# A hybrid encoder layer on one core: mixer preparation queued between the last pairs of the first way down, the mixer's second norm started later, some two-operand VectorE/POOL work moved to VectorE, and the closing norms regrouped

## Chip, cores, metric

The kernel runs on one core of one Trainium2 chip. A core has TensorE (PE in the profile; PEld is its weight loads), VectorE (DVE), ScalarE (ACT), GpSimd (POOL) and SyncE (SP), which here only issues transfers. The metric is device time in microseconds of a whole execution, as the median of several runs.

## The reference

One layer of a streaming encoder for 1152 tokens (1024 of a new stream, eight running streams of 16) with 1024 features, all in float32:

```python
x = x + 0.5 * swiglu(rms_norm(x, norm_ffn1), w_ffn1_gate, w_ffn1_up, w_ffn1_down)
m = mixer(rms_norm(x, norm_mix), w_in, ..., w_out, s0, conv_buf, pool_buf, pos0, chunk)
x = x + m
x = x + 0.5 * swiglu(rms_norm(x, norm_ffn2), w_ffn2_gate, w_ffn2_up, w_ffn2_down)
y = rms_norm(x, norm_final)
```

`swiglu` is `(silu(x @ w_gate) * (x @ w_up)) @ w_down` with 2816 hidden features. The mixer projects its input into a gated delta rule of four heads (causal convolution, normalised keys and queries, a chunked triangular solve, a state) and four pooled groups, and multiplies the joined result by `w_out`. The states are outputs too.

## The kernel before

Features lie on the 128 partitions (eight tiles of 128, `KT`), tokens along the free axis, in three chunks: chunk 0 of 512 tokens, chunks 1 and 2 of 320 each. To keep float32 accuracy at the matmul's faster type, each operand is split into a high part (ACT, a cast) and a low part (the difference), and each product is three matmuls: high x high, high x low, low x high. Nearly all of them are issued in `Products.matmul` (line 58), the transposes in line 62, so that these two lines stand for all of PE's work.

The program runs in this order.

1. `half_step` (first feed-forward half): gate and up projections. Chunks 1 and 2 are multiplied by 2x2 blocks of weights with seven block products instead of eight (Strassen's form); the sums of blocks that this needs are made in `Blocks.piece`: with two sources POOL adds them (L282), with `more` POOL adds a second sum to the first (L286), ACT makes the high part (L287), VectorE the low part (L288). `Blocks.mark` is the last low part issued, and `tc.issue_after(Blocks.mark)` queues what VectorE does in its block behind that instruction in VectorE's queue (order alone, no wait). The pieces turn round in a ring of buffers.
2. `downs`, the way down: `down0` for chunk 0, then `down12` for chunks 1 and 2 in twelve pairs `(g, d)`: the groups g have 4, 3 and 4 units ("four-wide", "three-wide"), and each has four pairs. A pair is seven products: `fifth` (T1), B11, B21, the T4 of the pair before, T2, B22, T3. Its four blocks of weights are loaded by SP into raw buffers that are reused (`load`, L642 and L643). `add` (L654) accumulates a product into x on VectorE. Of a pair's seven pieces three are sums of two blocks, T1's with `more`. A generator `beside` is advanced three times in a pair, after B21, B22 and T3; before the change it carries only the final norm of chunk 0, in the second way down.
3. The mixer. `h_tiles(0)` and `scale_split` (L249 on ACT, L250 on VectorE) make chunk 0's scaled input; `rstd_of` and `rstd_parts` square it (L205, ACT), sum the squares (L209, VectorE) and take the root. Chunk 0's norm is the slow form (`fast=False`): two matmuls with a matrix of ones, a square root on ACT (L217), a reciprocal on VectorE (L218). The fast form (`rstd_rest`) sums by tiny matmuls, scales on VectorE (L231), takes the power -1/2 on POOL (L232) and spreads the result with matmuls that ACT copies out (L237).
   The order within the mixer is made by a planner at build time. Tasks have names such as `Ay0`: block A (chunk 0) or B (chunks 1 and 2), a letter, a head. `p`, `v`, `g` are projections, `w` and `y` prepare and invert the triangular matrix, `c` runs the chain of states, `m` is a pooled group, `o` multiplies by the output weights, `r` is the second norm (chunks 1 and 2). `rule(n, ...)` names what must be done before n. A list `fill` of projections and output products is worked off in its order, and a task at its head that isn't free yet stops it; the other tasks are taken when they are due: a step that yields t is due again after 1.35 t of the planned PE time. After that a scheduler puts each engine's instructions into an order of its own by priority and its estimate of when they are ready, so that work later in the program may run earlier.
   `load_mix` loads and splits a 128 x 1024 block of weights (L185 the high part on ACT, L186 the low part): the low part is VectorE's, but POOL's for the output weights (kind "o", sixteen blocks).
   The inverse's first part is a loop of thirty small VectorE steps (L1120, L1121); its last copies are in L1173. Output products are added to x in L1002.
4. The second half step and way down. In the last pairs `square` squares each finished tile of x (L1552, ACT) and sums (L1558, VectorE); the last square of a chunk is kept apart. After the last product `final(2)` and `final(1)` run step by step in turn: sums, power, spread, then eight scalings each: VectorE straight from PSUM (L1579), two of eight on POOL (L1577, after a multiplication by the weight on ACT, L1576), and each tile is stored by SP or ACT (L1583). `final(0)` runs beside the first pairs and scales in L1582.

Of the kernel before, what the change touches and what calls it, by code (L numbers as in the profile page):

```python
# [40 lines left out]
def trunk(ctx: ExitStack, tc: tile.TileContext, xin, s0, convst, poolst, cm_in, vec_in, small_in,  # L41
# [5 lines left out]
    class Products:  # L47
# [3 lines left out]
        def put(self, r, time):  # L51
            self.t += time

# [135 lines left out]
    def load_mix(src, kind):  # L189
        with tc.high_priority(offset=300):  # L190
            return load_unit(src, None, G if kind in "o" else V)
# [76 lines left out]
    class Blocks:  # L268


        def __init__(self, ring):
            self.gs, self.ring, self.n = Slots(), ring, 0

        def piece(self, *src, more=None):
# [5 lines left out]
            if len(src) == 2:  # L280
                t = self.gs.get("s", m)
                G.tensor_add(t, *src)  # L282
                src = [t]
# [328 lines left out]
    def down12(wd, gk, op0, beside, done):  # L612


        bl = Blocks(["O3", "O4", "O0", "O1", "O2"])
        gs, piece, product = bl.gs, bl.piece, bl.product
# [53 lines left out]
        for u, (g, d) in enumerate(units):  # L670
# [76 lines left out]
    def downs(wd, gk, src, done0=None, after=lambda c: (), done12=None):  # L747
# [65 lines left out]

    half_step(0, wg1, wu1, g_keep)
    downs(wd1, g_keep, xin)


    weights(("R0", "R1", "O5"), (("O2", "O3"), ("O4", "O6"), ("O0", "O1")))
    ms = Slots()
    mt = ms.get  # L820
    WIDE = HIST + 512 + NB * (HIST + NS)
# [6 lines left out]
    ms.place(region("A4"), ("raw", WIDE, 2), ("ss", 32, 2), ("sss", 32, 2), ("ucar", 60, 1), ("cst", 288, 1))  # L828
# [4 lines left out]
    ms.place(region("R2"), ("eglS", 32, 1), ("osbs", P, 1), ("scout", 288, 1), ("Vcs", 16, 2), ("Ucs", 16, 1), ("tus", 16, 1))  # L833
    ms.place(region("R3"), ("big", 1024, 1))
# [35 lines left out]
    R = [mt("big", 512), rb[:, :320], rb[:, 320:]]  # L870
    ROWS = ((0, 1, 2, 0), (1, 0, 2, 1))

    def mix_block(blk, hb, extra, zrow):
# [471 lines left out]
        def part_of(w, h):  # L1345
# [42 lines left out]
            if w == "r":  # L1388
                sq = mt("z", 640)
                for c in (1, 2):  # L1390
                    rstd_of(c, pair(z2, sq[:, :320], sq[:, 320:]), R[c], True)
                yield 1
        return part_of

    def pair(acc, *sq):
# [3 lines left out]
        def get(tag):  # L1399
            if tag == "nacc":  # L1400
                return acc
            turn[0] += 1
            return sq[turn[0] % 2]
# [80 lines left out]
    rule("Am0", "Ar0")  # L1484
# [57 lines left out]
    def square(c, d):  # L1542
# [17 lines left out]
    def final(c):  # L1560
        o, n = CHUNKS[c]
        last = c > 0
        pool = (2, 5) if last else ()
        r = nt[c].get("nsq", n)
        root = rstd_rest(n, squares[c], r)
        next(root)
        if not last:
            yield
            yield
        yield  # L1570
        pr = yield from root
        yield
        for k in range(KT):
            x, w = xk(c, k), vec[:, 24 + k:25 + k]
            if k in pool:
                A.mul(x, x, w)  # L1576
                G.tensor_tensor(x, x, r, ALU.mult)  # L1577
            elif last:
                V.scalar_tensor_tensor(x, x, w, pr, ALU.mult, ALU.mult)  # L1579
            else:  # L1580
                with tc.issue_after(Blocks.mark):
                    V.scalar_tensor_tensor(x, x, w, r, ALU.mult, ALU.mult)  # L1582
            (A if last and (k in pool or c == 1 and k % 2) else SY).dma_start(y_out[:, o * KT + k * n:o * KT + (k + 1) * n], x)  # L1583
            yield

    downs(wd2, g_keep, x_keep, lambda d: square(0, d), final, square)


# [90 lines left out]
```

## Time and profile before

| | |
|---|---|
| median of 3 runs | 2175.2 us (2174.64 to 2175.72) |
| the profiled execution's own time | 2173.01 us |
| its span in the profile | 2171.2 us |
| instructions | 33111 |
| PE busy | 2121.9 us, 98% of the span |
| VectorE busy | 1525.1 us, 70% |
| ACT busy | 924.8 us, 43% |
| POOL busy | 607.1 us, 28% |
| mean granted TensorE clock | 0.996 |

Times in the profile are microseconds from the start of the span, those of single groups nanoseconds. A row of the timeline is: start, duration, engine, line, operation, tile written and tiles read, shapes, count, and in brackets how long the engine had idled and whose end released it. "Busy" of PE is modelled, as matmuls overlap; a hole in it is real, a busy PE need not be at its peak. The final stores and the closing of the program lie behind the last computing instruction, inside the span.

### The profile page before, as it was taken

To read this page: it belongs to the slowest core of one execution; us is meant where nothing else is said; L and a number is where in the kernel's file an instruction comes from. 1 tells how busy PE (TensorE), PEld (TensorE's weight loads), DVE (VectorE), ACT (ScalarE), POOL (GpSimd) and SP (SyncE) were. 2 spreads that over 40 slices of the span, in tenths; PEclk is the share of its full clock that TensorE was granted. 3 is DMA by queue.
4 is the path that set the end of the run, shared out by engine and by line. 5 is a ranking of instruction groups with operands and counts; after the bars stand their busy time and mean duration, and the time that the engine had idled before them with its cause. 6 is when DMAs were issued, how large, how long until landed. Compare 5 with 4: busy or idle time off the path is not lost.

```text
span 2171.2 us, 33111 instructions
## 1 busy us (share of the span) xinstructions
PE 2121.9 (98%) x12341; PEld 1914.9 (88%) x12341; DVE 1525.1 (70%) x2764; ACT 924.8 (43%) x1886; POOL 607.1 (28%) x532
## 2 busy tenths in 40 slices
PE   8999999999999999999999999999999999999997
PEld 7899999999889887787899988889999999987997
DVE  7966666677337887778687877786666668744776
ACT  7433333444213455545455445543433334422333
POOL 1433333351014421111111211243333334100443
PEclk9999999999999999999999999999999999999998
DMA  6333333464465622121222122433333347446572
GB/s 254 117 124 107 127 113 110 164 222 144 152 217 196 232 78 79 40 69 51 71 90 81 54 87 91 165 117 114 117 112 122 111 141 245 137 134 220 201 263 70
DMA packets 102673, 289.71 MB, mean 133 GB/s; under 512 B 16240, under 2 KB 24304, under 8 KB 102256
## 3 DMA queue, kind: packets, MB, share of 16 engines
q1 hardware_dynamic: 101360, 286.40, 39.2%
q8 instruction: 97, 1.59, 0.3%
q10 hardware_dynamic: 1152, 1.19, 0.2%
q14 instruction: 64, 0.52, 0.1%
HBM read 214.89 MB, written 72.66 MB: 132 GB/s over the span
## 4 chain that ended last, share of the span: by engine, by line
PE 80%; DVE 10%; DMA 4%; issue 2%; ACT 2%; POOL 2%; SPq 0%; DVEq 0%; POOLq 0%; ACTq 0%
PE ps_a L58 29%; PE ps_b L58 19%; PE ps_d L58 17%; PE ps_c L58 14%; DVE O L288 2%; DMA R<-in_wd 1%; DVE x L654 1%; DMA B<-g_keep 1%; POOL Q L282 1%; DMA O<-in_wd 1%; PE ps_b L62 1%; DVE A L1120 1%; DVE A L1121 1%; ACT O L287 1%; DMA x<-g_keep 1%
## 5 line engine op out<-in xcount | busy, mean ns | idle before, releaser
L58 PE MATMUL ps_a<-B,O 128*128 128x320 f32 x3040 | 506.4, 310 | 9.6 <-DVE x L654 6.1
L58 PEld LDWEIGHTS ps_a<-B,O 128*128 128x128 f32 x3040 | 463.2, 188 | 21.2 <-issue 6.6
L58 PE MATMUL ps_a<-A,O 128*128 128x320 f32 (+1 forms) x1952 | 423.8, 353 | 5.6 <-DVE O L186 2.1
L58 PEld LDWEIGHTS ps_a<-A,O 128*128 128x128 f32 x1952 | 328.7, 189 | 40.1 <-issue 3.5
L288 DVE TENSOR_TENSOR O<-Q,O 128x512 fp32r<-128x512 f32 (+1 forms) x238 | 209.0, 879 | 194.2 <-ACT O L287 193.4
L58 PE MATMUL ps_b<-A,O 128*128 128x512 f32 (+1 forms) x1128 | 263.6, 387 | 6.3 <-ACT O L287 5.6
L58 PEld LDWEIGHTS ps_b<-A,O 128*128 128x128 f32 x1128 | 207.7, 188 | 46.9 <-ACT O L287 5.8
L58 PE MATMUL ps_d<-A,O 128*128 128x512 f32 x1056 | 244.0, 391 | 2.2 <-DVE x L606 1.3
L58 PEld LDWEIGHTS ps_d<-A,O 128*128 128x128 f32 x1056 | 196.8, 188 | 48.2 <-issue 3.5
L287 ACT CAST O<-Q 128x512 fp32r<-128x512 f32 (+1 forms) x238 | 143.3, 605 | 225.5 <-POOL Q L282 58.3
L288 DVE TENSOR_TENSOR O<-R,O 128x512 fp32r<-128x512 f32 (+1 forms) x216 | 199.3, 927 | 34.9 <-ACT O L287 33.9
L58 PE MATMUL ps_d<-B,O 128*128 128x320 f32 (+1 forms) x1104 | 203.8, 330 | 6.1 <-DVE x L1002 4.0
L58 PE MATMUL ps_c<-A,O 128*128 128x512 f32 (+1 forms) x816 | 186.9, 377 | 0.9 <-DVE O L288 0.9
L58 PEld LDWEIGHTS ps_d<-B,O 128*128 128x128 f32 x1104 | 171.1, 188 | 16.8 <-DVE x L1002 6.4
L287 ACT CAST O<-R 128x512 fp32r<-128x512 f32 (+1 forms) x216 | 131.2, 611 | 127.9 <-PE ps_a L58 50.2
L282 POOL TENSOR_TENSOR Q<-R 128x512 f32<-128x512 f32 (+1 forms) x44 | 57.7, 1311 | 450.1 <-DMA R<-in_wd 285.3
L58 PEld LDWEIGHTS ps_c<-A,O 128*128 128x128 f32 x816 | 145.5, 188 | 25.0 <-DVE O L288 1.4
L185 ACT CAST O<-R 128x1024 fp32r<-128x1024 f32 (+1 forms) x86 | 85.9, 1010 | 183.7 <-PE ps_d L58 134.7
L58 PE MATMUL ps_c<-B,O 128*128 128x320 f32 x912 | 145.5, 311 | 0.0
L58 PEld LDWEIGHTS ps_c<-B,O 128*128 128x128 f32 x912 | 137.8, 189 | 0.3
L186 DVE TENSOR_TENSOR O<-R,O 128x1024 fp32r<-128x1024 f32 (+1 forms) x74 | 87.2, 1185 | 50.5 <-ACT O L185 29.8
L393 POOL TENSOR_TENSOR A<-A,A 128x512 fp32r<-128x512 f32 x44 | 72.7, 1652 | 162.1 <-ACT A L392 162.0
(311 smaller groups left out, 2982.7 us busy)
## 6 DMA issues: line engine op xcount, KB each, us to landing
g_keep<-x SPq DMA_DIRECT2D x98, 320.0 KB, 2.5
R<-in_wg SPq DMA_DIRECT2D x48, 512.0 KB, 3.8
R<-in_wd SPq DMA_DIRECT2D x48, 512.0 KB, 3.7
R<-in_wu SPq DMA_DIRECT2D x47, 512.0 KB, 3.6
g_keep<-A SPq DMA_DIRECT2D x44, 512.0 KB, 2.7
A<-g_keep SPq DMA_DIRECT2D x44, 512.0 KB, 5.5
B<-g_keep SPq DMA_DIRECT2D x56, 320.0 KB, 6.6
A<-g_keep SPq DMA_DIRECT2D x42, 320.0 KB, 4.9
```

Source lines behind the costliest of these rows:

```text
L58: self.put(nc.tensor.matmul(out, lhs, rhs, **k), n / 2400 + .003 if lhs.dtype == F32R else max(n, lhs.shape[-1]) / 600)
L62: self.put(nc.tensor.transpose(out, lhs, rhs), out.shape[-1] / 1200)
L185: A.copy(hi, raw)
L186: (e or V).tensor_sub(lo, raw, hi.bitcast(F32))
L282: G.tensor_add(t, *src)
L287: Blocks.high = A.copy(hi, src).ins
L288: Blocks.mark = V.tensor_sub(lo, src, hi.bitcast(F32)).ins
L393: G.tensor_sub(go[:, 1], sg, go[:, 0].bitcast(F32))
L654: V.scalar_tensor_tensor(xk(c, d), ps, by, xk(c, d), ALU.mult, ALU.add)
L1120: V.tensor_tensor(tu[:, :n, :w], xrow(slice(None), m), Uc[:, :, m:m + 1].to_broadcast([P, n, w]), ALU.mult)
L1121: V.tensor_tensor(Uc[:, :, m + 1:], Uc[:, :, m + 1:], tu[:, :n, :w], ALU.add)
```

## The change

Five parts, none of which adds or removes a product of the layer.

- **Sums of blocks in the way down.** `Blocks` has an engine `e` for the sum of two sources, POOL as before. `down12` sets it to VectorE, and to POOL from the load of a three-wide pair to the load of the next four-wide one. The `more` sum stays on POOL.
- **Mixer preparation.** A generator `prologue` is given to the first way down as its `beside`: it lets 25 steps pass, then makes chunk 0's scaled input tile by tile, each followed by its square (`step=1`), VectorE's part queued behind the latest piece, with 2, 3, 3, 1, 1 and 1 steps in between; what is left comes after the last pair. This norm now has the fast form. Its square's buffer is one of the `raw` slots in place of `z`.
- **Second norm.** `Ar0` must wait for `Ay0`, and `Am1` for `Ar0` (before, `Am0` for `Ar0` and `Ar0` for nothing). It is cut into steps, each due after a yield of 2, and has one square's buffer of its own (`sqr`).
- **Low parts of the output weights** are made by VectorE as all others.
- **The end.** The last products' chunks have their seven first squares summed as soon as chunk 2's last tile is done (`partial`); `finals` adds the eighth, takes both powers, then spreads and scales chunk 2 and then chunk 1, tiles 1, 4 and 7 on POOL, stores of odd tiles on ACT's queue and of even ones on SP's. `final0` waits three steps before its root and takes two steps per tile.

```diff
-            return load_unit(src, None, G if kind in "o" else V)
+            return load_unit(src)
...
-                G.tensor_add(t, *src)
+                self.e.tensor_add(t, *src)
...
         bl = Blocks(["O3", "O4", "O0", "O1", "O2"])
+        bl.e = V
...
+                bl.e = G if GROUPS[g2][1] == 3 else V
                 w = load(g2, d2, 6 if g2 == 0 else 10)
...
-        down12(wd, gk, op0, iter(after(0)), done12)
-
-        ends = [iter(after(c)) for c in (2, 1)]
-        while ends:
-            ends = [e for e in ends if next(e, e) is not e]
+        down12(wd, gk, op0, iter(after0()), done12)
+        ends()
...
+    def prologue():
+
+        for _ in range(25):
+            yield
...
+        hb0.extend(h_tiles(0))
+        R.append(mt("big", 512))
+        buf = [mt("raw", 512) for _ in range(2)]
+        norm = rstd_parts(0, lambda tag: buf[tag == "nsq"], R[0], step=1)
+        for k in range(KT):
+            with tc.issue_after(Blocks.mark):
+                scale_split(0, 1, *hb0, [k])
+                next(norm)
+            for _ in range((2, 3, 3, 1, 1, 1, 0, 0)[k]):
+                yield
+        yield from norm
+
     half_step(0, wg1, wu1, g_keep)
-    downs(wd1, g_keep, xin)
+    downs(wd1, g_keep, xin, after0=prologue)
...
             if w == "r":
-                sq = mt("z", 640)
                 for c in (1, 2):
-                    rstd_of(c, pair(z2, sq[:, :320], sq[:, 320:]), R[c], True)
-                yield 1
+                    for _ in rstd_parts(c, pair(z2, mt("sqr", 320)), R[c], step=1):
+                        yield 2
...
-    hb = {0: h_tiles(0)}
-    scale_split(0, 1, *hb[0])
-    rstd_of(0, pair(mt("raw", 512), mt("raw", 512), mt("z", 512)), R[0], False)
+    hb = {0: hb0}
...
-    rule("Am0", "Ar0")
+    rule("Ar0", "Ay0")
+    rule("Am1", "Ar0")
...
             squares[c].append(t)
+            if c == 2:
+                partial(2)
+                partial(1)
...
+    def final0():
+
+        r = nt[0].get("nsq", N0)
+        root = rstd_rest(N0, squares[0], r)
+        next(root)
+        for _ in range(3):
+            yield
+        yield from root
+        yield
+        for k in range(KT):
+            with tc.issue_after(Blocks.mark):
+                t = scaled(0, k, r, V)
+            SY.dma_start(*t)
             yield
             yield
...
+    def finals():
+
+        root = {}
+        for c in (2, 1):
+            ss = pt("d")[:, :3]
+            for i, a in enumerate(AT):
+                T.matmul(ss[:, i:i + 1], squares[c][1][:, a:a + P], ones[:, 0:1], start=True, stop=True)
+            summed = T.last
+            root[c] = const.tile([P, 4], F32, tag="rt", name=nm("rt"), bufs=3)[:, :3]
+            V.scalar_tensor_tensor(root[c], ss, 1.0 / D, sums[c], ALU.mult, ALU.add)
+            G.tensor_tensor(root[c], root[c], mhalf[:, :3], ALU.pow)
+        for c in (2, 1):
+            pr, r = pt("d")[:, :N], nt[c].get("nsq", N)
+            with tc.issue_after(summed):
+                for i, a in enumerate(AT):
+                    T.matmul(pr[:, a:a + P], root[c][:, i:i + 1].to_broadcast([P, P]), ident, start=True, stop=True)
+            A.copy(r, pr)
+            for k in range(KT):
+                pool = k in (1, 4, 7)
+                t = scaled(c, k, r if pool else pr, G if pool else V)
+                (A if k % 2 else SY).dma_start(*t)
...
-    downs(wd2, g_keep, x_keep, lambda d: square(0, d), final, square)
+    downs(wd2, g_keep, x_keep, lambda d: square(0, d), final0, square, finals)
```

`partial(c)` sums `squares[c][0]` with three tiny matmuls and scales the result on VectorE; `scaled` is a multiplication by weight and root, in one instruction on VectorE, or on ACT and then POOL.

More of the change, by code (lines that the diff above doesn't have):

```diff
@@ L52, in put @@
             self.t += time
+            self.last = r.ins
         def matmul(self, out, lhs, rhs, **k):
@@ L745, in half_step, with downs @@
         rest()
-    def downs(wd, gk, src, done0=None, after=lambda c: (), done12=None):
+    def downs(wd, gk, src, done0=None, after0=lambda: (), done12=None, ends=lambda: None):
         op0, stage = {}, []
```

54 lines of the change are left out of this document (25 added, 29 removed).

## The prediction

> **What bounds the kernel now.** I read the page first, then the table by stretches (busy time of each engine between two times) for the stages that the change touches, then the chain that ended last and the timeline inside them.
>
> ```profile
> PE 2121.9 (98%) x12341; PEld 1914.9 (88%) x12341; DVE 1525.1 (70%) x2764; ACT 924.8 (43%) x1886; POOL 607.1 (28%) x532
> ```
>
> TensorE (PE) is busy for 98% of the span, so no edit that leaves its matmuls alone can gain more than the holes between them. In the next two tables the first time is the width of the stretch and the second is PE's busy time in it; the time after the count is the weight loads', and then come VectorE (DVE), ACT and POOL. The first table is the way down of the two feed-forward halves after its first chunk (three rows each: four-wide, three-wide and four-wide group, roughly), the second the mixer.
>
> ```profile
> 653.00:694.00 41.00, 40.57 (x275) 40.05 (x274) 28.41 (x47) 14.44 (x25) 18.39 (x14) 1.00 0.48 160
> 694.00:738.00 44.00, 42.66 (x286) 41.59 (x285) 35.62 (x64) 19.94 (x38) 17.33 (x16) 1.00 0.84 308
> 738.00:788.00 50.00, 46.20 (x300) 45.21 (x299) 44.33 (x70) 21.68 (x37) 22.45 (x16) 0.97 0.28 91
> 1998.00:2047.00 49.00, 47.44 (x300) 45.24 (x300) 32.70 (x49) 15.37 (x27) 19.48 (x13) 1.00 0.64 215
> 2047.00:2104.00 57.00, 54.31 (x362) 53.11 (x363) 42.17 (x80) 17.49 (x35) 21.77 (x20) 1.00 0.74 266
> 2104.00:2153.00 49.00, 46.63 (x315) 45.72 (x314) 39.62 (x65) 22.91 (x43) 19.16 (x14) 1.00 0.15 44
> ```
>
> ```profile
> 800.00:877.00 77.00, 74.63 (x392) 60.73 (x391) 58.18 (x131) 47.12 (x100) 10.13 (x21) 1.00 0.23 66
> 877.00:932.00 55.00, 51.08 (x294) 42.68 (x293) 42.11 (x107) 26.39 (x78) 8.01 (x8) 0.97 0.14 44
> 932.00:1012.00 80.00, 76.68 (x410) 61.53 (x409) 65.04 (x166) 40.25 (x100) 16.90 (x19) 1.00 0.21 61
> 1012.00:1240.00 228.00, 226.71 (x1544) 209.77 (x1543) 178.25 (x539) 115.68 (x297) 38.30 (x72) 1.00 0.24 73
> 1240.00:1372.00 132.00, 124.20 (x848) 114.34 (x846) 98.96 (x258) 65.61 (x165) 21.58 (x21) 1.00 0.30 96
> ```
>
> Holes on PE, width less busy: 0.43 + 1.34 + 3.80 = 5.57 us in the first way down, 1.56 + 2.69 + 2.37 = 6.62 in the second, 2.37 + 3.92 + 3.32 + 1.29 + 7.80 = 18.70 in the mixer. In the same rows VectorE is the second engine: 44.33 of 50 us in the last pairs of the first way down. A hole can also cost a slower clock behind it (third column from the end):
>
> ```profile
> 738.00:745.00 7.00, 4.11 (x27) 3.59 (x25) 6.86 (x8) 2.42 (x5) 6.92 (x5) 1.00 0.27 107
> 745.00:749.50 4.50, 4.50 (x21) 4.50 (x22) 4.03 (x9) 3.12 (x5) 1.01 (x1) 0.62 0.45 125
> ```
>
> After 2.89 us idle within seven, PE runs the next 4.5 us at 0.62 of its clock: 4.5 x 0.38 = 1.71 us more, so the first way down has 7.28 us to win. The Trainium skill (TensorE: Matmul & The Clock Gate, What's actually happening) lets the clock fall only after an idle window of some 3.4 us; this trace shows it falling after less, so I follow the trace. By the page, the 1.71 us would not hang on this hole, and the estimate below would be 0.9 us smaller.
>
> **Way down: sums on VectorE.** What ends the waits there is told by the chain in the second way down (start, us, what), and the matmul that it releases:
>
> ```profile
> 2040.37 1.31 POOL Q L282
> ...
> 2043.80 1.39 DVE O L288
> ...
> 2046.90 0.40 DVE x L654
> ```
>
> ```profile
> 2048.44 3.75 PE L58 MATMUL ps_a<-B,O 128*128 128x320 f32 x24 [1.66 <-DVE x L654]
> ```
>
> Weights land, POOL adds two of them (1.31), ACT makes the high part, VectorE the low part (1.39), and the accumulation that PE needs (L654) stands behind all that in VectorE's queue. The groups of VectorE between 738 and 788 us show what the low parts cost beside POOL (count | busy us, mean ns of one):
>
> ```profile
> L288 DVE TENSOR_TENSOR O<-A,O 128x512 fp32r<-128x512 f32 x15 | 15.9, 1063 | 2.5 <-ACT O L287 2.3
> L288 DVE TENSOR_TENSOR O<-R,O 128x512 fp32r<-128x512 f32 x4 | 2.7, 678 | 0.0
> ```
>
> The same instruction takes 678 ns alone and 1063 where POOL adds at the time. Per pair of four-wide units three of POOL's four sums move (POOL's fourth and the three-wide group's sums stay): 24 per way down, 48 in all, at 0.68 us each on VectorE (the row of L288 alone: the same operation on the same shape) instead of 1.31 on POOL. A four-wide pair has 7 products x 4 tiles x 3 matmuls = 84, so the last stretch holds 300/84 = 3.6 pairs: 10.7 sums, 7.3 us more on VectorE. Given back: 15 x 0.385 = 5.8 us on that row alone; with three of four POOL sums gone, three quarters of it, 4.3. Net +3.0 on 44.33, against PE's own need of 50 - 3.80 - 1.71 = 44.5: VectorE and PE are level there. In the second way down VectorE has 32.70 + 7.3 = 40 and 39.62 + 7.3 = 47 before anything is given back, against 47.4 and 46.6 of PE: room, and the chain per pair is shorter by 0.63 (sum) and up to 0.7 (low part) of its 1.66 us wait. New waits: VectorE's sum now waits for the weights' DMA; behind it in its queue stand the accumulations L654 and the low parts of the next piece, and PE waits for both. POOL's remaining sum now waits for VectorE's. As PE waits for the same landing through the split anyway, I count this as nothing; if not, rival 3.
>
> Preparation of the mixer (eight scaled splits and squares) is now queued behind chosen pieces of the last four pairs, one tile at a time, where the scheduler had put it wherever it was ready; the work is the same. Its last two tiles come after the last pair. What covers these is this product, the last of the way down, and the one before it:
>
> ```profile
> 791.57 2.00 PE L58 MATMUL ps_a<-B,O 128*128 128x320 f32 x12
> ```
>
> Without that cover two tiles would cost 2 x (0.68 + 0.68) = 2.7 us. Square root and reciprocal of the first norm go; no wait in the list of PE's waits hangs on them for long: nothing. The first chunk's final scaling takes two steps per tile instead of one and so reaches into the three-wide group, where PE has 2.69 us of holes and VectorE 42.17 of 57: nothing, 0.5 at worst.
>
> I take half of 7.28 in the first way down (3.6; VectorE is level with PE), 60% of 6.62 in the second (4.0). Ends: all of both (13.9), and rival 1.
>
> **Second norm.** Two of PE's waits at the mixer's start are its pieces, one on a square's sum, one on POOL's power; one of its sums on VectorE is the third row; the last two are the end of the first pair's inverse and the first product of Am1, the task that now must wait for the norm:
>
> ```profile
> 803.73 0.83 PE L58 MATMUL ps_d<-ones,B 128*128 128x1 f32 x6 [1.08 <-DVE B L209]
> 818.18 0.94 PE L58 MATMUL ps_d<-ident,rt 128*128 128x128 f32 x6 [1.05 <-POOL rt L232]
> 801.30 0.49 DVE L209 TENSOR_TENSOR B<-B,A 128x320 f32<-128x320 f32 x1
> 874.70 0.41 DVE L1173 COPY B<-ps_b 64x256 f32<-64x256 f32 x1
> 932.39 0.94 PE L58 MATMUL ps_a<-A,O 128*128 128x512 f32 x3
> ```
>
> Gained: 1.08 + 1.05 = 2.1. Moved: 16 squares and 14 x 0.49 = 6.9 us of VectorE land between about 877 and 932, where PE has 3.92 us of holes; I charge 1.0 (0 to 3).
>
> **Output weights' low parts.** Sixteen go from POOL to VectorE. Durations (min/median/max ns), then three instructions of one small VectorE loop and a split beside it:
>
> ```profile
> L186 POOL TENSOR_TENSOR O<-R,O x12: 2357/2410/2938, 886.6 to 1342.9; 128x1024 fp32r<-128x1024 f32 x12
> L186 DVE TENSOR_TENSOR O<-O,O x14: 1161/1222/1227, 794.7 to 1283.3; 128x1024 fp32r<-128x1024 f32 x14
> 895.53 0.20 DVE L1120 TENSOR_TENSOR A<-A,A 128x36 f32<-128x36 f32 x1
> 896.81 2.39 POOL L186 TENSOR_TENSOR O<-O,O 128x1024 fp32r<-128x1024 f32 x1
> 896.92 2.33 DVE L1120 TENSOR_TENSOR A<-A,A 128x28 f32<-128x28 f32 x1
> ```
>
> A 0.20 us step is held for 2.33 by the split: it costs VectorE 2.1 us without running there. On VectorE it costs 1.22. Added: 16 x 1.22 = 19.5; given back at most 16 x 2.1 = 34, at least nothing. The stretches with these splits hold 3.92 + 3.32 + 7.80 = 15.0 us of PE's holes. That is what they can win, and not all of it hangs on VectorE: I take a third, 5.0; ends 15 and -10 (rival 1).
>
> **End.** Sums of squares in two parts, the first ahead; both powers before both spreads; scaling divided 10 to 6 between VectorE and POOL instead of 12 to 4; SP and ACT issue eight stores each instead of nine and seven.
>
> ```profile
> 2156.12 0.47 ACT L1552 ACTIVATE A<-x 128x320 f32<-128x320 f32 x1 [2.20 <-DVE x L654]
> 2158.24 1.41 PE L58 MATMUL ps_d<-ones,A 128*128 128x1 f32 x10
> 2160.84 1.65 PE L58 MATMUL ps_d<-ident,rt 128*128 128x128 f32 x6 [0.55 <-POOL rt L232]
> 2160.33 0.42 ACT L237 COPY A<-ps_d 128x320 f32<-128x320 f32 x1 [3.73 <-PE ps_d L58]
> 2160.79 1.47 DVE L1579 SCALAR_TENSOR_TENSOR x<-x,vec,ps_d 128x320 f32<-128x320 f32 x3 [0.93 <-ACT A L237]
> 2163.04 4.21 DVE L1579 SCALAR_TENSOR_TENSOR x<-x,vec,ps_d 128x320 f32<-128x320 f32 x9 [0.79 <-ACT A L237]
> ```
>
> The last square ends at 2156.59; six small sums at 1.41/10 each take 0.85 (2157.4); the other chunk's power is then done, so its spread follows: 0.94 to 1.65, I take 1.3 (2158.7); then ACT's copy and a start, 0.46. First scaling at about 2159.2 instead of 2160.79, and 10 x 0.49 (1.47/3) = 4.9 without the pause: last at 2164.1 instead of 2167.25. The stores start with the first scaling, and if it is they that set the end, its 1.6 us is all there is; if the last scaling sets it, 3.1. I take 1.6 (0.5 to 3.1).
>
> **Sum.** 3.6 + 4.0 + 2.1 - 1.0 + 5.0 + 1.6 = 15.3 us. The profiled execution took 2173.0 (span 2171.2 and 1.8 around it), so 2157.7; the median of the runs shown is 2175.2, 2.2 above the profiled one, so 2159.9. A difference of 0.2% (4.4 us) is about what a measurement of this kernel can tell from none.
>
> **Rivals.**
> 1. VectorE becomes the bound, and it is slower. Place: the last four-wide pairs of the first way down and the mixer's chains. If nothing is given back, VectorE has 44.33 + 7.3 = 51.6 us in a stretch of 50 (+1.6), and half of the 19.5 us of splits stand in PE's way (+9.8); less 1.6 at the end and 1.1 of the norm, +8.7: 2183.9. It decides where the low parts still average above 900 ns with the sums on VectorE. For it: 89% busy there already. Against: 678 against 1063 ns. The Trainium skill (Perfetto Trace Analysis, Optimizing Scalar/DVE Operations) speaks for it: work should leave a saturated DVE, to GPSIMD if need be. Chance 0.07.
> 2. The norm blocks the mixer's filler. It takes 18 steps, each followed by 2 x 1.35 = 2.7 us in the plan, 48.6 in all, from 874.70 to about 924; Am1 starts at 932.39, and a task that isn't free stops the whole list of filler. Ten us late would cost some 7 of PE's time and a clock dip of 1.7: 2168.6. Chance 0.10.
> 3. The way down gives nothing: VectorE waits on landings with L654 behind it, and the holes stay. 2159.9 + 7.6 = 2167.5. Chance 0.17.
> 4. Nearly all goes: 13.9 in the way down and 10 in the mixer instead of 7.6 and 5.0: 2159.9 - 11.3 = 2148.6, or somewhat lower. Chance 0.11.
> 5. Gains and new waits cancel: 2171 to 2179. The Trainium skill (the same page and section) holds that moving work between GPSIMD and DVE might not help, as they share a port. Chance 0.08.
>
> **How the numbers follow.** Forecast 0.47, at 2159.9. Faster: it and rivals 2, 3 and 4, less 0.03 for the slow tails of 2 and 3: 0.82. Same: 0.08 and those 0.03, 0.11. Slower: 0.07. The range 2146 to 2173 leaves out rival 1, half of 5 and a little of 4, under 0.2.
>
> **What the changed profile would show.** Right: L288 at 0.7 us in both ways down; PE's hole and clock dip at 742 gone; no wait of PE on L209 or L232 at 800 to 820; single steps of L1120 at 0.2 us throughout; the first scaling 1.6 us earlier behind the last product. Wrong: VectorE at 46 or more of 46 us in the last pairs; holes of several us before Am1; longer waits behind L186 on VectorE.

## The result and the profile after

The changed kernel takes 2148.84 us (median of 4 runs, 2147.65 to 2149.61), the kernel before beside it 2175.01 (4 runs, 2174.64 to 2175.72): ratio 0.9879, 95% interval 0.9862 to 0.9896. That is 26.2 us less; 15.3 were forecast. The profiled execution took 2148.53 us, its span is 2146.7. In the code after, lines have moved: the low part L288 is L289, the sum L282 is L283, the accumulation L654 is L656, the split L186 is L187, the loop L1120 is L1139, the products' L58 is L59.

The page's line of engines after. Against before TensorE has lost 5.6 us of busy time (2121.9 before), its holes shrink from 2171.2 - 2121.9 = 49.3 us to 30.4, VectorE is as busy as it was, and POOL has lost 109 us:

```profile
PE 2116.3 (99%) x12355; PEld 1914.3 (89%) x12355; DVE 1528.7 (71%) x2828; ACT 925.8 (43%) x1886; POOL 498.4 (23%) x471
```

The table by stretches of the two ways down after (start and end, width, then busy time of PE, its weight loads, VectorE, ACT, POOL, and the clock), to be held against the six rows of the prediction:

```profile
645.40:685.00 39.60, 39.60 (x270) 39.48 (x269) 33.99 (x57) 14.69 (x24) 4.81 (x4) 1.00 0.61 211
685.00:729.00 44.00, 43.41 (x294) 42.89 (x293) 33.22 (x61) 17.13 (x34) 16.64 (x16) 1.00 0.80 289
729.00:786.40 57.40, 56.47 (x375) 54.26 (x374) 54.30 (x98) 29.95 (x50) 6.48 (x6) 1.00 0.37 116
1989.00:2038.00 49.00, 49.00 (x339) 48.92 (x338) 42.01 (x73) 18.73 (x32) 10.70 (x8) 1.00 0.60 200
2038.00:2094.00 56.00, 54.04 (x356) 52.01 (x355) 44.51 (x83) 19.43 (x38) 15.65 (x14) 1.00 0.74 266
2094.00:2132.20 38.20, 38.20 (x264) 37.96 (x263) 31.45 (x60) 18.46 (x35) 2.60 (x2) 1.00 0.15 42
```

PE's holes: 1.52 us where 5.57 were, and 1.96 where 6.62 were. VectorE is at 54.30 of 57.40 us in the last pairs, 95%, and PE is held there for less than 1 us. The mixer in the same view:

```profile
787.00:862.00 75.00, 74.16 (x389) 59.70 (x389) 56.88 (x133) 43.79 (x92) 7.94 (x20) 1.00 0.24 72
862.00:917.00 55.00, 54.81 (x322) 46.22 (x321) 45.16 (x116) 30.38 (x86) 5.42 (x7) 1.00 0.15 49
917.00:995.00 78.00, 77.14 (x422) 63.34 (x421) 62.81 (x162) 41.03 (x102) 6.79 (x16) 1.00 0.21 63
995.00:1223.00 228.00, 227.27 (x1551) 209.97 (x1550) 181.91 (x552) 116.13 (x296) 27.32 (x68) 1.00 0.24 73
1223.00:1352.70 129.70, 123.30 (x835) 114.03 (x835) 97.52 (x262) 64.72 (x164) 8.68 (x15) 0.99 0.31 98
```

Holes of 9.0 us instead of 18.7. VectorE's busy time over these rows is 444.3 us, before 442.5. The rows are not quite the same work, as the preparation now lies ahead of them; the cleaner count is that of the low parts alone (b_olow, next section): over the whole mixer VectorE is busy for 445.5 us there and for 448.2 before. Sixteen splits were added, 19.5 us by the forecast's count, and all of it was given back by steps that are held no longer. In the small loop this is plain (count, then min/median/max ns); the first line is of before, the second of after:

```profile
L1120 DVE TENSOR_TENSOR A<-A,A x120: 155/187/2427, 840.8 to 1309.8; 128x60 f32<-128x60 f32 x8, 128x56 f32<-128x56 f32 x8, 128x52 f32<-128x52 f32 x8, 128x48 f32<-128x48 f32 x8
```

```profile
L1139 DVE TENSOR_TENSOR A<-A,A x120: 153/188/275, 827.4 to 1289.3; 128x60 f32<-128x60 f32 x8, 128x56 f32<-128x56 f32 x8, 128x52 f32<-128x52 f32 x8, 128x48 f32<-128x48 f32 x8
```

PE's waits on the accumulation, over the whole kernel (us in total, times, longest), before and after:

```profile
PE ps_a L58 <- DVE x L654: 7.2, 10, 1.7
```

```profile
PE ps_a L59 <- DVE x L656: 1.4, 2, 0.7
PE ps_d L59 <- DMA A<-in_wpool: 2.1, 1, 2.1
```

The second row of after is a wait on the landing of a 64 KB load, which before did not have. Every kernel here with the output weights' low parts on VectorE has it (2.0 to 2.5 us) and none of the others: it is a new cost of that part, and no run shows why it comes. In after it leaves the one hole behind which the clock still falls in the mixer:

```profile
1310.00:1312.60 2.60, 0.48 (x4) 0.30 (x3) 0.99 (x3) 0.00 (x0) 0.00 (x0) 1.00 0.91 345
1312.60:1316.00 3.40, 3.38 (x11) 2.62 (x12) 0.35 (x1) 1.16 (x4) 0.00 (x0) 0.53 0.83 272
```

The end after, from the timeline:

```profile
2130.43 2.00 PE L59 MATMUL ps_a<-B,O 128*128 128x320 f32 x12
...
2132.99 0.47 ACT L1569 ACTIVATE A<-x 128x320 f32<-128x320 f32 x1 [2.22 <-DVE x L656]
...
2135.62 4.67 DVE L1588 SCALAR_TENSOR_TENSOR x<-x,vec,ps_d 128x320 f32<-128x320 f32 x10 [1.07 <-ACT A L1634]
2135.66 4.96 POOL L1586 TENSOR_TENSOR x<-x,A 128x320 f32<-128x320 f32 x6 [0.18 <-ACT A L1634]
2136.19 6.81 SPq L1638 DMA_DIRECT2D out_y<-x  x8
```

Lengths of the six stages, from PE's products in each trace (us): the way up of the first half with the loads, the first way down, the mixer, the second way up, the second way down, and from the end of the last product to the end of the span. The kernels are those of the next section. Each is one execution: where the code is the same, a stage still differs by up to some 3 us (the first by 646 to 649, the second way down by 146.7 in before and 149.2 in b_prep), so only differences beyond that, or seen in several kernels, are used.

| kernel | up | down | mixer | up | down | end | span |
|---|---|---|---|---|---|---|---|
| before | 646.4 | 147.2 | 578.1 | 637.1 | 146.7 | 15.7 | 2171.2 |
| after | 646.1 | 140.6 | 566.3 | 636.5 | 143.1 | 14.3 | 2146.7 |
| b_sums | 646.4 | 140.1 | 579.1 | 636.3 | 140.8 | 15.5 | 2158.2 |
| b_olow | 646.9 | 148.0 | 567.0 | 637.1 | 147.2 | 15.5 | 2161.6 |
| b_norm | 648.7 | 147.7 | 573.6 | 637.1 | 147.1 | 15.7 | 2169.8 |
| b_prep | 648.6 | 144.2 | 579.6 | 637.3 | 149.2 | 16.9 | 2175.8 |
| b_three | 647.0 | 139.8 | 565.3 | 636.9 | 140.4 | 15.5 | 2144.9 |
| b_three_all | 647.4 | 139.9 | 565.1 | 636.2 | 140.4 | 16.9 | 2146.0 |
| a_no_end | 648.0 | 140.2 | 564.8 | 636.8 | 140.4 | 17.1 | 2147.3 |
| a_no_norm | 647.3 | 139.8 | 568.3 | 636.8 | 142.6 | 13.9 | 2148.6 |
| a_pool_read | 647.5 | 140.3 | 587.0 | 637.0 | 143.0 | 14.1 | 2168.9 |
| a_pool_write | 648.5 | 140.5 | 564.9 | 637.0 | 142.6 | 14.6 | 2148.0 |
| s_read | 649.0 | 160.2 | 580.3 | 638.1 | 159.5 | 15.5 | 2202.8 |
| s_write | 649.5 | 139.3 | 580.3 | 636.2 | 140.6 | 15.5 | 2161.4 |

### The profile page after: what moved, and what is told of

The parts are those of the page before. It is cut to its first block, busy times and chain, and to the rows that moved or that the text cites. A ratio compares the mean times of both kernels' runs of the same rounds, so it can differ in the third digit from the quotient of the medians.

```text
span 2146.7 us, 33093 instructions
## 1 busy us (share of the span) xinstructions
PE 2116.3 (99%) x12355; PEld 1914.3 (89%) x12355; DVE 1528.7 (71%) x2828; ACT 925.8 (43%) x1886; POOL 498.4 (23%) x471
## 4 chain that ended last, share of the span: by engine, by line
PE 89%; DVE 5%; DMA 3%; ACT 1%; POOL 1%; issue 1%; SPq 0%; POOLq 0%; DVEq 0%; ACTq 0%
PE ps_a L59 33%; PE ps_b L59 21%; PE ps_d L59 18%; PE ps_c L59 16%; DVE O L187 1%; DMA B<-g_keep 1%; PE ps_b L63 1%; DMA x<-g_keep 1%; DVE O L289 0%; DVE B L1000 0%; DVE B L769 0%; ACT O L186 0%; DVE A L1139 0%; DVE A L1140 0%; DVE x L656 0%
## 5 line engine op out<-in xcount | busy, mean ns | idle before, releaser
L59 PE MATMUL ps_a<-B,O 128*128 128x320 f32 x3040 | 504.5, 309 | 0.3
L59 PEld LDWEIGHTS ps_a<-B,O 128*128 128x128 f32 x3040 | 463.3, 188 | 9.1 <-issue 0.8
L59 PE MATMUL ps_a<-A,O 128*128 128x320 f32 (+1 forms) x1952 | 424.4, 352 | 1.7 <-DVE x L656 1.4
L59 PEld LDWEIGHTS ps_a<-A,O 128*128 128x128 f32 x1952 | 328.1, 188 | 35.3 <-ACT O L288 1.8
L289 DVE TENSOR_TENSOR O<-Q,O 128x512 fp32r<-128x512 f32 (+1 forms) x238 | 199.4, 840 | 175.6 <-ACT O L288 174.6
L59 PE MATMUL ps_b<-A,O 128*128 128x512 f32 (+1 forms) x1128 | 263.9, 387 | 5.8 <-ACT O L288 5.8
L59 PEld LDWEIGHTS ps_b<-A,O 128*128 128x128 f32 x1128 | 208.0, 188 | 46.2 <-ACT O L288 6.0
L59 PE MATMUL ps_d<-A,O 128*128 128x512 f32 x1056 | 244.2, 391 | 1.6 <-DVE x L607 0.4
L59 PEld LDWEIGHTS ps_d<-A,O 128*128 128x128 f32 x1056 | 196.8, 188 | 47.8 <-ACT O L186 3.0
L288 ACT CAST O<-Q 128x512 fp32r<-128x512 f32 (+1 forms) x238 | 143.1, 605 | 201.2 <-PE ps_c L59 54.7
L289 DVE TENSOR_TENSOR O<-R,O 128x512 fp32r<-128x512 f32 (+1 forms) x216 | 196.3, 912 | 35.7 <-ACT O L288 34.8
L59 PE MATMUL ps_d<-B,O 128*128 128x320 f32 (+1 forms) x1104 | 201.8, 329 | 1.8 <-ACT B L1027 1.0
L288 ACT CAST O<-R 128x512 fp32r<-128x512 f32 (+1 forms) x216 | 131.4, 611 | 144.9 <-PE ps_a L59 56.7
L59 PE MATMUL ps_c<-A,O 128*128 128x512 f32 (+1 forms) x816 | 187.2, 377 | 1.0 <-DVE O L289 1.0
L59 PEld LDWEIGHTS ps_d<-B,O 128*128 128x128 f32 x1104 | 171.2, 188 | 11.0 <-DVE x L1021 2.0
L59 PEld LDWEIGHTS ps_c<-A,O 128*128 128x128 f32 x816 | 145.5, 188 | 25.3 <-DVE O L289 1.8
L186 ACT CAST O<-R 128x1024 fp32r<-128x1024 f32 (+1 forms) x86 | 85.9, 1010 | 168.5 <-PE ps_d L59 127.7
L59 PE MATMUL ps_c<-B,O 128*128 128x320 f32 x912 | 144.8, 309 | 0.6 <-DVE O L289 0.6
L59 PEld LDWEIGHTS ps_c<-B,O 128*128 128x128 f32 x912 | 136.6, 188 | 1.3 <-DVE O L289 0.9
L187 DVE TENSOR_TENSOR O<-R,O 128x1024 fp32r<-128x1024 f32 (+1 forms) x86 | 101.7, 1189 | 49.2 <-ACT O L186 30.0
L59 PE MATMUL ps_b<-B,O 128*128 128x320 f32 x720 | 116.2, 309 | 0.0
```

The lines of the kernel that those rows point to most:

```text
L59: self.put(nc.tensor.matmul(out, lhs, rhs, **k), n / 2400 + .003 if lhs.dtype == F32R else max(n, lhs.shape[-1]) / 600)
L186: A.copy(hi, raw)
L187: (e or V).tensor_sub(lo, raw, hi.bitcast(F32))
L288: Blocks.high = A.copy(hi, src).ins
L289: Blocks.mark = V.tensor_sub(lo, src, hi.bitcast(F32)).ins
```

## The experiments

The theory after the result: the gain comes from POOL reading less while VectorE works. A step of VectorE with both sources in SBUF is held as long as POOL reads; the two moves take such reading away in the ways down and in the mixer. Its rivals: the shorter chain per pair (no sum on POOL ahead of the high part), POOL's queue being free, and the other three parts (norm, preparation, end).

**Each part alone, on the kernel before.** The sums (b_sums):

```diff
-            self.gs, self.ring, self.n = Slots(), ring, 0
+            self.gs, self.ring, self.n, self.e = Slots(), ring, 0, G
...
-                G.tensor_add(t, *src)
+                self.e.tensor_add(t, *src)
...
+        bl.e = V
...
+                bl.e = G if GROUPS[g2][1] == 3 else V
```

> The kernel before with the sums of two blocks in the way down on VectorE (POOL keeps them in the three-wide group), nothing else. Theory (POOL's reading holds VectorE's two-source steps, so a sum moved to VectorE costs it little): the second way down shortens by 3 to 4 us and the first by 2 to 4, in all 5 to 8 us; L288 falls from 1063 ns towards 700 in the last pairs. Rival (VectorE becomes the bound there): no gain or up to 2 us slower, L288 still above 900 ns. Rival (the gain of the way down came from the queued preparation alone): second way down unchanged within 0.5 us.

Measured: 2159.58 us beside 2174.93, ratio 0.9933 (0.9918 to 0.9948): 15.4 us less, about twice the 5 to 8 expected. The ways down lose 7.1 and 6.0 us, together 13.1, the mixer nothing. The last pairs' low parts, by shape (count, busy us, mean ns), took 1039 ns before where POOL adds; here:

```profile
L288 DVE TENSOR_TENSOR O<-A,O 128x512 fp32r<-128x512 f32 x16 | 11.6, 732 | 0.0
```

The low parts of the output weights (b_olow):

```diff
-            return load_unit(src, None, G if kind in "o" else V)
+            return load_unit(src)
```

> The kernel before with the low parts of the output weights on VectorE, nothing else. Theory: the mixer's shortening of about 12 us is mostly this, 6 to 10 us, and the steps of L1120 held for over 2 us are gone. Rival (the mixer gained by the second norm's new place): 0 to 2 us. Rival (sixteen times 1.22 us more on VectorE stands in PE's way): slower by 2 to 10 us.

Measured: 2164.45 us, 0.9958 (0.9941 to 0.9974): 10.5 less, all of it in the mixer (11.1). The loop's longest step falls from 2427 to 272 ns; of the long hole at 902 us 1.1 us is left, and the slow clock behind it is gone.

The second norm (b_norm):

```diff
-                sq = mt("z", 640)
                 for c in (1, 2):
-                    rstd_of(c, pair(z2, sq[:, :320], sq[:, 320:]), R[c], True)
-                yield 1
+                    for _ in rstd_parts(c, pair(z2, mt("sqr", 320)), R[c], step=1):
+                        yield 2
...
-    rule("Am0", "Ar0")
+    rule("Ar0", "Ay0")
+    rule("Am1", "Ar0")
```

> The kernel before with the second norm after Ay0, in steps, and Am1 behind it; nothing else. Theory: 2.1 us of PE's waits go, and up to 1 comes back later, so 1 to 2 us faster. Rival (this is where the mixer's gain comes from): 5 us or more faster. Rival (the filler list stops at Am1): slower by 2 to 9 us, with a hole on PE before Am1.

Measured: 2169.95 us, 0.9981 (0.9971 to 0.9990): 5.0 less, 4.5 of it in the mixer: not the 1 to 2 expected, but the first rival's 5. Two waits of 2.1 us in all go, as forecast; the rest is near 902 us. Before, holes of 2.98 us stand there and half a clock behind them. With the norm moved they are still there, a little earlier and shorter (1.29 + 0.87 us), but the slow clock, worth 1.7 us, is not. First before, then b_norm (third column from the end: the clock):

```profile
895.00:902.00 7.00, 7.00 (x39) 5.94 (x38) 6.72 (x17) 2.39 (x6) 2.68 (x3) 1.00 0.24 68
902.00:906.30 4.30, 1.40 (x8) 0.77 (x7) 3.99 (x16) 3.11 (x12) 0.00 (x0) 1.00 0.04 13
906.30:909.70 3.40, 3.32 (x10) 2.73 (x11) 2.68 (x11) 1.61 (x6) 1.38 (x1) 0.51 0.50 154
```

```profile
895.00:902.00 7.00, 5.71 (x33) 4.78 (x31) 6.93 (x19) 2.96 (x6) 3.03 (x3) 1.00 0.22 75
902.00:910.00 8.00, 7.13 (x44) 6.11 (x45) 7.38 (x23) 7.66 (x23) 1.04 (x1) 1.00 0.21 67
```

A slow stretch can stay away by chance (last section), but here it does so on average: the mean granted clock over all runs is 0.9960 with the norm moved and 0.9952 before, 1.7 us in 2171.

The preparation (b_prep):

```diff
     half_step(0, wg1, wu1, g_keep)
-    downs(wd1, g_keep, xin)
+    downs(wd1, g_keep, xin, after=lambda c: prologue() if c == 0 else ())
...
-    hb = {0: h_tiles(0)}
-    scale_split(0, 1, *hb[0])
-    rstd_of(0, pair(mt("raw", 512), mt("raw", 512), mt("z", 512)), R[0], False)
+    hb = {0: hb0}
```

> The kernel before with the mixer's preparation in the generator beside the last four pairs, and the first norm in its fast form; nothing else. Theory: POOL's sums still hold VectorE, so little of the first way down's 7 us comes back, 1 to 3 us, and another 1 to 2 at the mixer's start from the reciprocal that goes. Rival (the bunching alone made the hole at 742 us and the slow clock): 5 us or more, the hole and the slow clock gone with POOL's sums in place.

Measured: 2174.28 us, 0.9996 (0.9987 to 1.0005): nothing, as the prediction had it, and not the 2 to 5 us expected above. In its trace the first way down is 3.0 us shorter, but other stages are longer by as much and more. The profiled execution took 2177.56 us, 3.3 above that median; in it the slow clock behind the hole near 905 us lasts 6.8 us, where before has 3.4:

```profile
905.00:911.80 6.80, 5.95 (x19) 4.98 (x20) 3.45 (x11) 4.91 (x14) 1.38 (x1) 0.51 0.24 77
```

**Giving POOL its reading back.** After each of the sixteen output weights' splits of the kernel after, POOL subtracts a spare tile of 960 columns that nobody uses (a_pool_read), or fills it (a_pool_write). Work is added, none left out.

```diff
+    spare = const.tile([P, 960], F32, tag="spare", name="spare")
...
+        G.tensor_sub(spare, raw[:, :960], hi[:, :960].bitcast(F32))
```

> The kernel after; at each of the sixteen output-weight blocks POOL does as well what it did before the change, a subtraction that reads both parts (960 of the 1024 columns), into a spare tile that nobody reads. VectorE makes the low part that counts. Theory (POOL's reading holds VectorE's steps with two SBUF sources): 5 to 11 us slower than after, steps of L1139 and L1140 held for over 2 us again. Rival (what gained was the low part's own shorter time, 1.22 instead of 2.41 us): 0 to 1 us slower, since that stays.

```diff
+        G.memset(spare, 0.0)
```

> As the run with the spare subtraction, but POOL only fills the spare tile with zeros, so that it writes and reads nothing. Theory (reading is what holds VectorE): within 1 us of the kernel after. Rival (any long POOL instruction holds VectorE): slower, in the proportion of its shorter time, 2 to 5 us.

Measured: 2170.94 us with the reading, 0.9985 (0.9975 to 0.9994) of before; 2149.03 with the filling, 0.9883 (0.9868 to 0.9898), as after. The mixer takes 587.0 and 564.9 us, the other stages are alike. So 16 unused subtractions on an engine that is idle most of the time cost 22 us, beyond the 5 to 11 expected: four of VectorE's own splits, which start while the spare step reads, take 2.4 to 3.3 us instead of 1.2, and single steps of the loop take 2.25 us again. POOL's spare instructions (count, busy us, mean ns) and the loop's in each, reading first:

```profile
L195 POOL TENSOR_TENSOR spare<-R,O 128x960 f32<-128x960 f32 x12 | 34.7, 2890 | 40.1 <-issue 32.4 <-ACT O L186 7.5 <-ACT A L964 0.2
L1146 DVE TENSOR_TENSOR A<-A,A 128x60 f32<-128x60 f32 (+14 forms) x120 | 26.8, 223 | 2.3 <-ACT A L1131 0.9
```

```profile
L195 POOL MEMSET spare<- 128x960 f32 x16 | 14.4, 898 | 1.2 <-POOLq L1715 0.3
L1146 DVE TENSOR_TENSOR A<-A,A 128x60 f32<-128x60 f32 (+14 forms) x120 | 22.8, 190 | 2.3 <-ACT A L1131 1.0
```

The filling is also shorter (14.4 against 47.7 us in all), so the pair differs in more than reading. But what grows is VectorE's own busy time: over the mixer 468.29 us with the reading, 444.96 with the filling and 444.83 in after, 1222 instructions each time. Those 23.3 us cover the 22.1 that the mixer is longer by. Were POOL's being busy the cause, the fill would have added some 7 us (23.3 x 14.4/47.7); it added 0.1. Reading first:

```profile
787.80:1374.90 587.10, 562.14 (x3520) 496.55 (x3518) 468.29 (x1222) 296.13 (x740) 102.56 (x142) 0.99 0.23 72
789.00:1353.90 564.90, 555.54 (x3518) 492.58 (x3518) 444.96 (x1222) 296.15 (x740) 55.98 (x126) 1.00 0.24 75
```

PE's longer waits in a_pool_read end mostly on VectorE (4.5 us on L1028 alone, 0.7 us on the same line after), none of the longer ones on POOL.

The same in the ways down, on b_sums: beside each sum that VectorE took over, POOL makes a spare one of the same sources (s_read), or fills a tile of the same size (s_write).

```diff
                 self.e.tensor_add(t, *src)
+                if self.e is V:
+                    G.tensor_add(spare[:, :m], *src)
```

> The kernel before with the way down's sums on VectorE, and beside each moved sum a spare one on POOL: POOL reads the same two weights again and writes a tile that nobody uses. Work is added, none is left out. Theory A: the 15.4 us of the sums alone come from POOL no longer reading while VectorE makes the low parts; then the spare sums take most of it back, and VectorE, which now also has the sums, is held in those too: 2170 to 2185, the low parts L288 (a line or two lower here) back at 1000 ns, the two ways down at 145 to 150 us each instead of 140. Theory B: they come from the shorter chain (no 1.3 us sum and no hand-over from POOL ahead of the high part); then the spare sums cost little: 2160 to 2165.

```diff
                 self.e.tensor_add(t, *src)
+                if self.e is V:
+                    G.memset(spare[:, :m], 0.0)
```

> The same with a spare fill of the same size on POOL in the place of the spare sum: POOL only writes a tile that nobody uses. Both theories: about as the sums alone, 2160, both ways down at 140 to 142 us. Were it longer by 5 us or more, it would be POOL's being busy, or its queue, and not its reading that costs.

Measured beside 2175.39: 2203.54 us with the reading, 1.0129 (1.0114 to 1.0144), and 2162.48 with the filling, 0.9944 (0.9929 to 0.9958). The reading costs 41 us over the filling, beyond the 2185 that theory A gave at most: the ways down take 160.2 and 159.5 us, with the filling 139.3 and 140.6. The last pairs in s_read, VectorE by shape: low parts, accumulations (one source in PSUM), the input's scaling, the moved sums, and last in a fence of its own s_write's low parts:

```profile
L291 DVE TENSOR_TENSOR O<-A,O 128x512 fp32r<-128x512 f32 x16 | 16.6, 1038 | 0.0
L658 DVE SCALAR_TENSOR_TENSOR x<-ps_a,x 128x320 f32<-128x320 f32 x20 | 9.6, 481 | 0.8 <-PE ps_a L58 0.8
L251 DVE SCALAR_TENSOR_TENSOR A<-x,vec,A 128x512 fp32r<-128x512 f32 x8 | 8.8, 1118 | 0.0
...
L283 DVE TENSOR_TENSOR A<-A,R 128x512 f32<-128x512 f32 x2 | 3.1, 1572 | 0.0
L283 DVE TENSOR_TENSOR A<-R,R 128x512 f32<-128x512 f32 x2 | 3.0, 1492 | 0.0
```

```profile
L291 DVE TENSOR_TENSOR O<-A,O 128x512 fp32r<-128x512 f32 x16 | 11.7, 734 | 0.0
```

In these rows low parts, scaling and sums, all with two sources in SBUF, take 1.0 to 1.6 us in the mean (with the filling 0.7, 0.9 and 0.7 to 1.2); the accumulation, which reads one source from PSUM, stays at 481 ns (483). Every low part of these rows above 0.8 us, in before, in after and in s_read, lies over an addition of POOL. The Trainium skill (SBUF — State Buffer, Who interferes with whom) states just this: a DVE instruction with two SBUF inputs contends with a GpSimd instruction that reads SBUF and not with one that only writes it, and one with at most one SBUF input doesn't contend, outside the 2-port perf modes. Both pairs of runs agree. A longer queue on POOL, or weight buffers that come free later, is not what costs: VectorE is busy for 70.97 of the last 74.30 us of the first way down while PE has 10 us of holes, and PE's waits in the two ways down end on VectorE, but for 3.0 us on ACT:

```profile
735.00:809.30 74.30, 64.11 (x398) 60.45 (x398) 70.97 (x104) 34.94 (x59) 27.27 (x19) 0.95 0.34 106
```

Some 8.5 of the 41 us are slow clock (in the ways down 17.1 us at half). So POOL's reading is a cost of this size; whether the shorter chain adds to b_sums' 15.4 us isn't told apart, since there is no run that has POOL's sum in the chain and not its reading.

**What the other parts are worth together.** Before with sums, low parts and norm alone (b_three: the three diffs above), and after with the old end (a_no_end: before with those three and the preparation).

> The kernel before with three parts: sums on VectorE, output weights' low parts on VectorE, second norm later; neither the queued preparation nor the new end. Theory (these three carry the change; preparation and end nothing): within 2 us of after. If the three add up as measured alone (15.4 + 10.5 + 5.0), 2144. Rival (the preparation matters once VectorE is full of sums): 4 us or more slower than after, with a hole in the last pairs of the first way down.

> All but the new end: before with sums, low parts, second norm and preparation. Theory (the new end gains 1.2 us behind the last product, and its slower scaling of chunk 0 and earlier sums of squares give up to 2 back in the second way down): within 1.5 us of after either way, second way down 141 us instead of 143. Rival (the end is worth its forecast): 1.6 to 3 us slower than after.

The edit of a_no_end, against after:

```diff
-    downs(wd2, g_keep, x_keep, lambda d: square(0, d), final0, square, finals)
+    downs(wd2, g_keep, x_keep, lambda d: square(0, d), final, square)
```

Measured beside 2174.27: 2147.33 us, 0.9875 (0.9859 to 0.9892), and 2147.91, 0.9877 (0.9863 to 0.9892). Neither differs from after: preparation and end are worth nothing that can be measured. With the old end the second way down takes 140.4 to 140.8 us (five kernels) instead of 142.6 to 143.1 (four), and the end 15.5 to 17.1 instead of 13.9 to 14.6.

After with the norm as it was (a_no_norm), and b_three with the three-wide group's sums on VectorE too (b_three_all):

```diff
+                sq = mt("z", 640)
                 for c in (1, 2):
-                    for _ in rstd_parts(c, pair(z2, mt("sqr", 320)), R[c], step=1):
-                        yield 2
+                    rstd_of(c, pair(z2, sq[:, :320], sq[:, 320:]), R[c], True)
+                yield 1
...
-    rule("Ar0", "Ay0")
-    rule("Am1", "Ar0")
+    rule("Am0", "Ar0")
```

> The kernel after with the second norm as it was before (all its squares and powers at once ahead of the mixer's filler, Am0 waiting for it). Theory A (the terms add): 5.0 slower than after, as the norm alone gained 5.0: 2154. Theory B (the norm alone won mostly a hole and a clock dip near 906 us, which the low parts on VectorE remove too): 1 to 2.5 slower, the two waits of PE at 800 to 820 us alone: 2150 to 2151.

```diff
-                bl.e = G if GROUPS[g2][1] == 3 else V
```

> The kernel before with three parts of the change (sums, second norm, output weights' low parts), without the queued preparation and the new end, and with the three-wide group's sums on VectorE too: 48 to 60 more sums of 0.68 us. If VectorE at 97% in the last pairs is no bound, 2146 to 2148, as the three parts were (2147.3); if POOL's sums in the three-wide group still hold the low parts there, 1 to 3 us better; if VectorE is at its end there, 2 to 5 worse.

Measured beside 2175.39: a_no_norm 2151.85 us, 0.9894 (0.9879 to 0.9909), 23.5 less than before where after is 26.2 less; the intervals overlap, but the mixer is 2.0 us longer, and the waits at its start are back (1.5 us on a square's sum, 0.8 on POOL's power). That is nearer to theory B, though the time alone does not exclude theory A's 2154 (the interval reaches to 2155.6): alone the norm wins 5.0 us, on top of the low parts between 2 and 3, as the slow clock behind 902 us, which either of them removes, can be won only once. The three single gains, 15.4 + 10.5 + 5.0 = 30.9, are 3.9 more than b_three's 26.9 (2174.27 - 2147.33), which fits; with intervals of 2 to 4 us on each it is no proof. b_three_all takes 2148.05 us, 0.9878 (0.9861 to 0.9894): the 24 sums more on VectorE (72 instead of 48; the 48 to 60 expected were a miscount) neither win nor cost. No version is measurably better than after.

## Why the prediction was right in sign and too small

The time came out inside the range, near its low end, and at rival 4's size: 2148.6 against 2148.84. That the two agree to 0.2 us is luck: rival 4 had 13.9 us in the ways down and 11.1 in the mixer, where after has 10.2 (6.6 + 3.6) and 11.8.

- **What bounds it: right.** PE's products are what they were; 18.9 us of the span's 24.5 come from holes and 5.6 from PE's busy time, in which the slow stretches at 745 and 906 us are gone.
- **The way down: mechanism right, term mis-sized.** Forecast 3.6 + 4.0 = 7.6; measured alone 7.1 + 6.0 = 13.1, nearly all of the 13.9 that were there. The step that failed is "PE and VectorE are level there", from which I took half. By that sum VectorE would even have stood 2.8 us above PE (44.33 + 3.0 against 44.5). What was mis-sized in it is what comes back: over about the same last work of the first way down VectorE's busy time rose by 0.8 us (48.95 before, 49.77 in b_sums) and not by 3.0, so of the 7.3 us of sums some 6.5 were given back and not 4.3. Level they are (54.30 of 57.40 us beside PE's 56.47), but VectorE can be that full without PE waiting: what PE waited for were single steps that stood late in VectorE's queue while POOL read, and these went. VectorE busy through nearly all of the last pairs was a sign I had named as speaking against the forecast; it came, almost, and meant nothing by itself. Nor does the slow clock at 745 us share in a discount: it went as a whole.
- **The sign to look for, L288 at 0.7 us:** nearly. The median is 679 ns in the last pairs and the mean 868, as the sixteen low parts there still meet some additions of POOL, the `more` sums (the longest takes 1623):

```profile
L289 DVE TENSOR_TENSOR O<-A,O x16: 672/679/1623, 734.7 to 775.6; 128x512 fp32r<-128x512 f32 x16
```

- **Output weights: mechanism right, term mis-sized.** "Not all of it hangs on VectorE: I take a third", 5.0 of 15.0 us of holes. Alone it is 10.5; in after, together with the norm, the mixer's holes lost 9.7. The clock's fall at 906 us, which the sum left out, is another 1.7, and the new wait on a landing (2.1 us, with a fall of its own in after) is a cost that it left out too. The row that decided it was in the prediction: 0.20 us held for 2.33.
- **Second norm: right place, mis-sized.** +2.1 came; the charge of 1.0 did not, and 2.4 to 2.9 us more came near 902 us when it was tried alone, most of it the slow clock. I had looked at PE's holes near the norm's new place as a cost and not asked what the new order would win there. Which of the moved steps did that wasn't tried. Rival 2 fell: Am1's first product starts 133 us behind the mixer's start (919.71 against 786.4), before 139 (932.39 against 793.6).
- **Preparation: right,** nothing that can be measured (b_prep, and b_three beside a_no_end).
- **The end: right steps, no net.** From the last square to the first scaling 2.16 us instead of 4.20 (forecast 1.6 less), the last scaling 3.5 us earlier, and the span's end 1.4 earlier behind that square (13.2 against 14.6 us). That the stores set it, as I took, fits: the last one is issued at 2143.0 us, 2.4 behind the last scaling. No run tests it. But the small sums put ahead of the last product take 1.47 us there instead of 0.58, and L656's waits in the second way down are 1.4 us instead of the 0.3 with the old end; the second way down grows by about what the end wins. The step that failed is the cost of what is moved ahead, which I put at nothing.
- **Rivals.** Rival 1's mechanism is real, but it needs POOL reading beside: s_read is that case, low parts at 1038 ns and 2203.5 us. In after the mean is below its 900 ns. Rival 3 fell: PE's waits on landings did not come back in the ways down. Rival 5 fell. The Trainium skill's sentence (Perfetto Trace Analysis, Optimizing Scalar/DVE Operations) that moving work between these two engines might not help because of the shared port does not hold here: moving it gained 15.4 and 10.5 us. Where VectorE's steps have two sources in SBUF, that the two engines hold each other up is a reason to move work off POOL.

## What to carry to other kernels

Before a cost of an engine is put at its busy share, look at the longest durations of its short steps (here 0.2 us steps held for 2.3): they show who holds it, and the work that holds it is dear even on an idle engine. An engine at 95% of a stretch can take that work over, if what it gives up in held steps is as much as what it takes on, and if its steps that another engine waits for come early enough. Two edits that remove the same hole or the same slow stretch win it only once. A slow clock behind a hole belongs to its price, but isn't behind every such hole.

## What was not expected of the hardware

- POOL's reading costs far more than its length where VectorE runs steps with two SBUF sources: 47.7 us of spare reads cost the mixer 22 us, and 48 spare sums 40 us in the two ways down (319.7 us against 279.9 with fills). POOL's own additions lengthen too: the shortest spare ones of this size take 1.30 us, most 1.6 to 1.8. Fills of 14.4 and 25.0 us cost nothing in the same stages.

```profile
L285 POOL TENSOR_TENSOR spare<-R,R 128x512 f32<-128x512 f32 x8 | 13.0, 1622 | 0.6
```

- PE's clock falls to half for 3.4 us, in b_prep and b_olow once for 6.8. In after and before it falls behind holes of 2.1 and 2.9 us (2.60 us with 0.48 of work, 4.30 with 1.40). The length of the hole does not decide alone: in a_no_end the same wait as in after, 2.3 us, has the full clock behind it:

```profile
1312.00:1314.40 2.40, 0.11 (x2) 0.04 (x1) 0.74 (x2) 0.00 (x0) 0.00 (x0) 1.00 0.95 370
1314.40:1318.00 3.60, 3.60 (x24) 3.28 (x25) 1.19 (x4) 1.59 (x5) 0.00 (x0) 1.00 0.75 242
```

  In s_write it falls at 801.7 us with no hole above 1.1 us ahead of it. In every trace with more than one slow stretch their starts lie whole multiples of 3.413 us apart: in before 745.91 and 906.34 (47 of them), in a_pool_read 1005.33, 1333.01 and 1346.66 (96 and 4). So whether a hole costs these 1.7 us depends also on how it lies on this grid, which no edit here controls. The Trainium skill (TensorE: Matmul & The Clock Gate, What's actually happening) has the clock fall after an idle window of about 3.4 us: the length of the slow stretch agrees with that window, the length of the hole ahead of it does not.
